# FFNs and output projections with activations held in the array and 512 weight columns streamed, instead of weights held and tokens streamed

## The chip, the core and the metric

One NeuronCore of a Trainium2 chip runs the whole program. The metric is device microseconds of one execution; a comparison takes the median of several. Engines: PE multiplies matrices, DVE (VectorE) and ACT (ScalarE) work on elements, POOL prepares constants, SP issues DMAs. A matmul holds 128 x 128 numbers in the array (the stationary operand, loaded first) and streams the columns of the other (the moving operand) past them; its result goes to PSUM.

## The reference

A trunk of two layers over 256 tokens of 1024 channels, in float32. Layer 0 mixes tokens by latent attention and a spatial gate, layer 1 by a short gated convolution; each mixer stands between two FFNs, so there are four FFNs.

```python
def rms_norm(x, g):
    y = x32 * lax.rsqrt(jnp.mean(x32 * x32, axis=-1, keepdims=True) + NORM_EPS)
    return (y * g.astype(jnp.float32)).astype(x.dtype)

def swiglu(h, w_gate, w_up, w_down):           # 1024 -> 2816 -> 1024
    return (jax.nn.silu(h @ w_gate) * (h @ w_up)) @ w_down

for layer in range(DEPTH):
    x = x + 0.5 * swiglu(rms_norm(x, ffn_pre_norm[layer]), ...)
    h = rms_norm(x, mix_norm[layer])
    x = x + (mla_sgu_mixer(h, ...) if layer % 2 == 0 else short_conv_mixer(h, ...))
    x = x + 0.5 * swiglu(rms_norm(x, ffn_post_norm[layer]), ...)
return rms_norm(x, final_norm)
```

## The kernel before

Activations stay on the chip with channels on partitions and the 256 tokens on the free axis. Every float32 operand of a large product is split into two parts, hi and lo (float32r), and three of the four products of parts are made: hi x hi, hi x lo, lo x hi. ACT makes hi by a copy (`whi`, line 123), DVE makes lo by a subtraction (`wlo`, line 126); the activation's two parts lie side by side as `[hi | lo]`, 512 columns (`mv` for x times a norm's gain, `a` for silu's result).

Weights come in pieces of 1 MB (2048 numbers on each partition) in the order of their use, `plan`. `prefetch` issues a piece's DMA on SP three pieces ahead of its use and splits it; raw, hi and lo have three buffers each.

Where a tile of 128 weight columns is held, `mm` (lines 164 and 165) makes a pair: w_hi against all 512 columns of `[a_hi | a_lo]`, then w_lo against the 256 of a_hi. `mm3` (lines 169 to 171) makes the same as a triple of three 256-column products into one half bank. An FFN (`ffn`) runs over 22 tiles f of 128 hidden channels: `products(f)` makes gate and up (8 tiles of channels x 2 x a pair), then `gate(f - 1)` adds the two halves (`pair_sum`), multiplies by the norm's factor spread over the partitions, applies silu and splits the result into `a[f]`. `project_out` runs four times over 256 output channels: 22 x 2 pairs each, and triples in the last of the four, then adds into x. The mixers' output projections use the same function. A norm takes squares of x (ACT), adds them up (DVE), sums over partitions on PE (line 211), takes the root, and for an FFN spreads the factor again on PE (line 221). At the end x is turned by 16 transposes and written.

One product already stands the other way, with tokens on partitions and 512 weight columns streamed: the gate's v and the attention's values (`natural`, lines 583 to 585).

A scheduler sets each engine's order from the data dependences and priorities (`tc.high_priority()`); an engine then works in that order and waits at whatever is not ready.

Of the kernel before, what the change touches and what calls it, by code (L numbers as in the profile page):

```python
# [63 lines left out]
def trunk(ctx: ExitStack, tc: tile.TileContext, io: dict, out: bass.AP, stop=None):  # L64
# [26 lines left out]
    plan += [io["e_out"][c] for c in range(4)]  # L91
# [4 lines left out]
    plan += [io["c_out"][c] for c in range(4)]  # L96
# [4 lines left out]
    def prefetch(n):  # L101
        while len(ready) < min(n, len(plan)):
            src = plan[len(ready)]
            w = src.shape[1]
# [4 lines left out]
            cuts = [0, 256, 512, 1024, 1536, w] if n == 0 else list(range(0, w, 512)) + [w] if n == 1 else [0, w]  # L109
            pieces = list(zip(cuts, cuts[1:]))  # L110
            for a, b in pieces:
                if n == 0:
                    k0, k1 = a // 256, b // 256
                    c = k0 // 2
                    nc.sync.dma_start(x[c][:, k0 - 2 * c:k1 - 2 * c, :], io["xT"][:, k0:k1, :])
                nc.sync.dma_start(raw[:, a:b], src[:, a:b])
            for a, b in pieces:
                if n == 0:
                    for k in range(a // 256, b // 256):
                        split_to(mv[k], x[k // 2][:, k % 2, :], col(C_PRE0 + k))  # L120
                for q in range(a, b, HI_STEP):
                    e = slice(q, min(q + HI_STEP, b))
                    A.activation(hi[:, e], raw[:, e], AF.Copy)  # L123
                for q in range(a, b, LO_STEP):
                    e = slice(q, min(q + LO_STEP, b))
# [11 lines left out]
    # ---------------------------------------------------------------- input, small parameters  # L137
    small = const.tile([P, NCOL], F32, name="small")
    x = [const.tile([P, 2, T], F32, name=f"x{c}") for c in range(4)]
# [27 lines left out]
    def mm3(ps, hi, lo, m, first, last):  # L167
        """All three products into ps[:, 0:256]."""
# [4 lines left out]
    def split_to(m, src, scale=None):  # L173
        """m = [hi | lo] of src (times a per-partition scale)."""
# [6 lines left out]
    def rsqrt(v, name):  # L181
        """v ** -0.5 in [P, 2], to float32's accuracy."""
# [13 lines left out]
    def after(later, earlier):  # L196
        """`later` is issued behind `earlier` on their engine."""
# [4 lines left out]
    def norm_split(c, gcol):  # L202
        """mv of x[c]: x * gain, split."""
        return [split_to(mv[k], x[c][:, k % 2, :], col(gcol + k)) for k in (2 * c, 2 * c + 1)][1]

    def total(accs, behind=None):
        """Sums over partitions (channels), the tokens on partitions: [P, 2]."""
# [9 lines left out]
    def spread(rn, behind=None):  # L217
        """[P, 2] of the tokens -> [P, T] in PSUM, the same on every partition."""
# [8 lines left out]
    def refine(root, h, y):  # L227
        """y = 1 / root, one Newton step further; h: -0.5 * what the root is of."""
# [7 lines left out]
    def rms(ps):  # L236
# [3 lines left out]
        A.activation(root, ps, AF.Sqrt, scale=1.0 / D, bias=eps)  # L240
# [138 lines left out]
    if stop == "f0":  # L379
        return dump()  # L380
# [422 lines left out]
```

## Time and profile before

| | us |
|---|---|
| median of 3 runs | 948.96 |
| lowest and highest | 947.68, 949.72 |
| the profiled execution, first to last instruction (span) | 949.5 |
| PE busy | 934.3 |
| DVE busy | 705.7 |
| ACT busy | 539.2 |

The page gives for the profiled execution its span alone, 0.5 us above the median of the runs. Busy times of PE are lengths of matmuls that overlap, so that PE looks busy even where it does not run at its best; the distance between two starts tells more. A group's row by form gives the count, the busy time, the mean length in ns, and the idle time before it with what ended that.

### The profile page before, as it was taken

How to read it: one execution, taken by the hardware profiler on the slowest of the kernel's cores; microseconds unless marked ns; L12 is line 12 of the kernel's file. 1: busy time of each engine (PE TensorE's matmuls, PEld its weight loads, DVE VectorE, ACT ScalarE, POOL GpSimd, SP SyncE). 2: the span in 40 equal slices, each digit the busy share in tenths (PEclk: the TensorE clock that was granted, in tenths of full speed). 3: DMA queues.
4: the chain of work that ended last, by engine and by line, in shares of the span. 5: the costliest groups of instructions: out<-in, count | busy, mean ns of one | idle time of the engine just before them, and what ended most of it. 6: DMA issues, size and time to landing. Idle time of an engine off the chain costs nothing.

```text
span 949.5 us, 14524 instructions
## 1 busy us (share of the span) xinstructions
PE 934.3 (98%) x5692; PEld 830.5 (87%) x5692; DVE 705.7 (74%) x1344; ACT 539.2 (57%) x827; POOL 4.6 (0%) x13
## 2 busy tenths in 40 slices
PE   7999999999999999999999999999999999999997
PEld 6888888998979888888998888889888888888887
DVE  6998775667778888775677887666788977788552
ACT  7655554554766655655456556554555665655542
POOL 0000000001000000000000000000000000000000
PEclk9999999999999999999999999999999999999999
DMA  8754455545415455555545555555455465555631
GB/s 278 275 208 178 177 193 174 197 170 177 178 49 190 177 206 178 183 195 174 203 178 188 205 184 181 196 173 205 178 183 208 149 214 177 188 205 174 200 122 45
DMA packets 26996, 173.60 MB, mean 183 GB/s; under 512 B 3120, under 2 KB 3760, under 8 KB 8240
## 3 DMA queue, kind: packets, MB, share of 16 engines
q1 hardware_dynamic: 26928, 172.68, 52.1%
q8 instruction: 44, 0.72, 0.3%
q14 instruction: 24, 0.20, 0.1%
HBM read 171.62 MB, written 1.05 MB: 182 GB/s over the span
## 4 chain that ended last, share of the span: by engine, by line
PE 96%; DVE 1%; ACT 1%; DMA 1%; SPq 0%; issue 0%; DVEq 0%; ACTq 0%
PE ps L164 53%; PE ps L165 27%; PE psb L171 3%; PE psb L170 3%; PE psb L169 3%; PE ps L170 1%; PE ps L171 1%; PE ps L169 1%; DMA x<-in_xT 1%; PE ps L583 0%; PE ps L584 0%; PE ps L585 0%; DVE wlo L126 0%; PE ps L651 0%; PE psb L221 0%; PE ps L673 0%
## 5 line engine op out<-in xcount | busy, mean ns | idle before, releaser
L126 DVE TENSOR_TENSOR wlo<-raw,whi 128x512 fp32r<-128x512 f32 (+1 forms) x647 | 430.6, 686 | 188.9 <-ACT whi L123 188.7
L164 PE MATMUL ps<-mv,whi 128*128 128x512 f32 x1600 | 561.9, 395 | 6.1 <-DVE mv L179 5.0
L123 ACT ACTIVATE whi<-raw 128x1024 fp32r<-128x1024 f32 (+2 forms) x337 | 337.9, 1018 | 213.1 <-PE ps L164 99.0
L165 PE MATMUL ps<-mv,wlo 128*128 128x256 f32 x1600 | 449.8, 281 | 0.3 <-DVE wlo L126 0.3
L164 PEld LDWEIGHTS ps<-mv,whi 128*128 128x128 f32 x1600 | 300.9, 188 | 74.3 <-ACT whi L123 6.6
L165 PEld LDWEIGHTS ps<-mv,wlo 128*128 128x128 f32 x1600 | 303.4, 190 | 1.2 <-DVE wlo L126 1.0
L164 PE MATMUL ps<-a,whi 128*128 128x512 f32 x624 | 218.0, 393 | 0.1
L165 PE MATMUL ps<-a,wlo 128*128 128x256 f32 x624 | 174.9, 281 | 0.0
L164 PEld LDWEIGHTS ps<-a,whi 128*128 128x128 f32 x624 | 116.9, 187 | 26.7 <-DVE a L177 0.4
L165 PEld LDWEIGHTS ps<-a,wlo 128*128 128x128 f32 x624 | 117.9, 189 | 0.2 <-issue 0.2
L359 ACT ACTIVATE silu<-pt 128x256 f32<-128x256 f32 x88 | 36.7, 418 | 95.3 <-DVE pt L357 95.3
L295 DVE TENSOR_TENSOR pt<-ps,sb 128x512 f32<-128x512 f32 x96 | 65.6, 683 | 0.5 <-ACT sb L294 0.4
L357 DVE TENSOR_TENSOR pt<-pt,r 128x512 f32<-128x512 f32 x88 | 60.2, 684 | 5.4 <-ACT r L270 5.3
L176 ACT ACTIVATE a<-pt 128x256 fp32r<-128x256 f32 x88 | 36.8, 418 | 41.8 <-DVE pt L360 41.8
L294 ACT ACTIVATE sb<-ps 128x512 f32<-128x512 f32 x100 | 58.1, 581 | 1.9 <-PE ps L165 1.9
L171 PE MATMUL psb<-a,wlo 128*128 128x256 f32 x208 | 58.8, 283 | 0.0
L170 PE MATMUL psb<-a,whi 128*128 128x256 f32 x208 | 58.8, 283 | 0.0
L169 PE MATMUL psb<-a,whi 128*128 128x256 f32 x208 | 58.8, 283 | 0.0
L169 PEld LDWEIGHTS psb<-a,whi 128*128 128x128 f32 x208 | 39.9, 192 | 0.3
L171 PEld LDWEIGHTS psb<-a,wlo 128*128 128x128 f32 x208 | 39.9, 192 | 0.0
L170 PEld LDWEIGHTS psb<-a,whi 128*128 128x128 f32 x208 | 39.9, 192 | 0.0
L177 DVE TENSOR_TENSOR a<-pt,a 128x256 fp32r<-128x256 f32 x88 | 36.9, 419 | 2.3 <-ACT a L176 2.2
(186 smaller groups left out, 546.0 us busy)
## 6 DMA issues: line engine op xcount, KB each, us to landing
raw<-in_f_gu SPq DMA_DIRECT2D x86, 1024.0 KB, 4.8
raw<-in_f_dn SPq DMA_DIRECT2D x32, 1024.0 KB, 4.9
raw<-in_f_dn SPq DMA_DIRECT2D x16, 768.0 KB, 4.2
raw<-in_c_cz SPq DMA_DIRECT2D x8, 1024.0 KB, 4.9
raw<-in_e_in SPq DMA_DIRECT2D x7, 1024.0 KB, 4.8
raw<-in_e_out SPq DMA_DIRECT2D x4, 1024.0 KB, 4.8
raw<-in_c_b SPq DMA_DIRECT2D x4, 1024.0 KB, 4.7
raw<-in_c_out SPq DMA_DIRECT2D x4, 1024.0 KB, 4.8
```

The costliest lines, as they stand in the source:

```text
L123: A.activation(hi[:, e], raw[:, e], AF.Copy)
L126: V.tensor_tensor(lo[:, e], raw[:, e], hi[:, e].bitcast(F32), ALU.subtract)
L164: PE.matmul(ps, lhsT=hi, rhs=m, start=first, stop=False)
L165: return PE.matmul(ps[:, :T], lhsT=lo, rhs=m[:, :T], start=False, stop=last)
L169: PE.matmul(ps, lhsT=hi, rhs=m[:, :T], start=first, stop=False)
L170: PE.matmul(ps, lhsT=hi, rhs=m[:, T:], start=False, stop=False)
L171: PE.matmul(ps, lhsT=lo, rhs=m[:, :T], start=False, stop=last)
L176: return (A.activation(m[:, :T], src, AF.Copy), V.tensor_tensor(m[:, T:], src, m[:, :T].bitcast(F32), ALU.subtract))
L177: V.tensor_tensor(m[:, T:], src, m[:, :T].bitcast(F32), ALU.subtract))
L294: A.activation(sb, ps[:, :, T:], AF.Copy)
L295: V.tensor_tensor(t, ps[:, :, :T], sb, ALU.add)
L357: V.tensor_tensor(t, t, bc(r[0], 2), ALU.mult)
```

## The change

In the four FFNs and the two output projections the operands change places: a 128-token half of the activations is held in the array, and 512 weight columns stream past. Results then have tokens on partitions. `mm_b` makes three products of 512 columns: a_hi with w_hi, a_hi with w_lo, a_lo with w_hi. `products(c)` now makes two tiles f at once (11 steps c), each with its own half of tokens in a PSUM bank; silu takes the norm's factor as a scale for each partition, and `gate` transposes the result on PE before it is split into `a`. x lies with tokens on partitions; `Norm.block` transposes each 512-column block of x as it comes out of `project_out`, splits it into `mv`, and takes its squares with a sum along the row. `project_out` holds four banks, keeps its last two pieces (TAIL) and finishes one block after the other. A piece of weights has the same size, but is cut over two tiles f and four tiles k, or over four groups of 256 columns. One instruction of DVE now splits 1024 columns, not 512.

```diff
-LOOKAHEAD = 3
-HI_STEP, LO_STEP = 1024, 512      # columns that one instruction splits
+LOOKAHEAD = 3
+TAIL = 2
+STEP = 1024
+NC = NF // 2
...
+    def down_plan(src, order):
+        v = src.rearrange("c p n -> p c n")
+        for i in order:
+            plan.append(v[:, :, i * 512:(i + 1) * 512])
...
-        for f in range(NF):
-            plan.append(io[f"{tag}_gu"][f])
-        for c in range(4):
-            for k0, k1 in ((0, 8), (8, 16), (16, 22)):
-                plan.append(io[f"{tag}_dn"][c][:, k0 * 256:k1 * 256])
+        v = io[f"{tag}_gu"].rearrange("f p n -> p f n")
+        for c in range(NC):
+            for h in range(2):
+                plan.append(v[:, 2 * c:2 * c + 2, h * 1024:(h + 1) * 1024])
+        down_plan(io[f"{tag}_dn"], range(NC))
...
+        def squares(self, h, b):
+            junk = work.tile([P, 512], F32, name="junk", tag="sq")
+            A.activation(junk, x[h][:, b * 512:(b + 1) * 512], AF.Square, accum_out=self.ss[:, b, h:h + 1])
+
+        def block(self, h, b):
+            if self.gcol is not None:
+                ps = psB.tile([P, 512], F32, name="psb")
+                for i in range(4):
+                    PE.transpose(ps[:, i * P:(i + 1) * P], x[h][:, b * 512 + i * P:b * 512 + (i + 1) * P], ident)
+                for i in range(4):
+                    k = 4 * b + i
+                    src, m, g = ps[:, i * P:(i + 1) * P], mv[k], col(self.gcol + k)
+                    hi, lo = m[:, h * P:(h + 1) * P], m[:, T + h * P:T + (h + 1) * P]
+                    A.activation(hi, src, AF.Copy, scale=g)
+                    V.scalar_tensor_tensor(lo, src, g, hi.bitcast(F32), ALU.mult, ALU.subtract)
+            self.squares(h, b)
...
+    def mm_b(ps, a, w, first, last):
+
+        PE.matmul(ps, lhsT=a[0], rhs=w[0], start=first, stop=False)
+        PE.matmul(ps, lhsT=a[0], rhs=w[1], start=False, stop=False)
+        PE.matmul(ps, lhsT=a[1], rhs=w[0], start=False, stop=last)
...
+        for i in order[:-TAIL]:
+            ws[i] = weights()
+            for h in range(2):
+                for b in range(2):
+                    step(i, h, b)
+        for i in order[-TAIL:]:
+            ws[i] = weights()
+        for b in range(2):
+            for h in range(2):
+                for i in order[-TAIL:]:
+                    step(i, h, b)
+                with tc.high_priority():
+                    xs = x[h][:, b * 512:(b + 1) * 512]
+                    V.scalar_tensor_tensor(xs, ps[h][:, b, :], s, xs, ALU.mult, ALU.add)
+                    norm.block(h, b)
...
+        def gate(c, ps):
+            s = work.tile([P, 2, 2, P], F32, name="silu")
+            for h in range(2):
+                v = ps[:, h, :].rearrange("p (f j n) -> p f j n", f=2, j=2)
+                A.activation(s[:, h], v[:, :, 0, :], AF.Silu, scale=rn[:, h:h + 1])
+                V.scalar_tensor_tensor(s[:, h], v[:, :, 1, :], rn[:, h:h + 1], s[:, h], ALU.mult, ALU.mult)
+            pt = psB.tile([P, 512], F32, name="psb")
+            for f in range(2):
+                for h in range(2):
+                    o = (2 * f + h) * P
+                    PE.transpose(pt[:, o:o + P], s[:, h, f, :], ident)
+            hi, lo = a[c]
+            A.activation(hi, pt, AF.Copy)
+            V.tensor_tensor(lo, pt, hi.bitcast(F32), ALU.subtract)
```

At the start x is turned by 16 transposes into the new lie. At the end the final norm needs no transposes: the gains are spread over the partitions once (`gain`, made by PE among the convolution's first products), and DVE multiplies x by factor and gain in four instructions, one for each output DMA.

Three places in the order of the built programs. First, PE in the middle of an FFN, where the products of one step end (on `mv7`) and those of the next begin (on `mv0`). Before:

```order
L165 MATMUL ps_1048<-mv6_101,wlo_987 128x256
L164 MATMUL ps_1048<-mv7_102,whi_986 128x512
L165 MATMUL ps_1048<-mv7_102,wlo_987 128x256
L164 MATMUL ps_1048<-mv7_102,whi_986 128x512
L165 MATMUL ps_1048<-mv7_102,wlo_987 128x256
L164 MATMUL ps_1101<-mv0_95,whi_1039 128x512
```

Now, the operand named first being the one that is streamed:

```order
L317 MATMUL ps_2760<-whi_2672,mv6_103 128x512
L315 MATMUL ps_2760<-whi_2672,mv7_104 128x512
L316 MATMUL ps_2760<-wlo_2673,mv7_104 128x512
L317 MATMUL ps_2760<-whi_2672,mv7_104 128x512
L315 MATMUL ps_2760<-whi_2672,mv7_104 128x512
L316 MATMUL ps_2760<-wlo_2673,mv7_104 128x512
L317 MATMUL ps_2760<-whi_2672,mv7_104 128x512
L374 MATMUL psb_2830<-ident_90,silu_2825 128x128 x4
L315 MATMUL ps_2837<-whi_2704,mv0_97 128x512
```

All products are of 512 columns now, and four transposes of the step before last stand between two steps.

Second, PE at the seam from the second FFN to the third: the last products of the down projection (on `a20`, `a21`) and the first of the next FFN (on `mv0`). Before:

```order
L169 MATMUL psb_4660<-a21_3083,whi_4641 128x256
L170 MATMUL psb_4660<-a21_3083,whi_4641 128x256
L171 MATMUL psb_4660<-a21_3083,wlo_4642 128x256
L164 MATMUL ps_4855<-mv0_95,whi_4650 128x512
L165 MATMUL ps_4855<-mv0_95,wlo_4651 128x256
```

Now:

```order
L315 MATMUL ps_3466<-whi_3692,a20_2603 128x512
L316 MATMUL ps_3466<-wlo_3693,a20_2603 128x512
L317 MATMUL ps_3466<-whi_3692,a21_2604 128x512
L315 MATMUL ps_3906<-whi_3724,mv0_97 128x512
L316 MATMUL ps_3906<-wlo_3725,mv0_97 128x512
L317 MATMUL ps_3906<-whi_3724,mv0_97 128x512
L315 MATMUL ps_3906<-whi_3724,mv1_98 128x512
L275 MATMUL psb_3868<-ident_90,x1_81 128x128 x4
L316 MATMUL ps_3906<-wlo_3725,mv1_98 128x512
```

The transposes of the last block of x (`x1`) stand four products into the next FFN; those of the three blocks ahead of it stand among the last products of the down projection.

Third, ACT at the same seam. Before, splits of x (`mv`, 256 columns) and squares (`sq`) among the splits of weights (`whi`):

```order
L123 ACTIVATE whi_4846<-raw_4845 128x1024 x2
L178 ACTIVATE mv6_101<-x3_83,small_79 128x256
L123 ACTIVATE whi_4889<-raw_4888 128x1024
L178 ACTIVATE mv7_102<-x3_83,small_79 128x256
L279 ACTIVATE sq_4820<-x3_83 128x512
```

Now (`psb` is the transposed block, `junk` takes the squares, `root` is the norm's root):

```order
L280 ACTIVATE mv4_101<-psb_3840,small_79 128x128
L139 ACTIVATE whi_3756<-raw_3755 128x1024
L280 ACTIVATE mv5_102<-psb_3840,small_79 128x128
L139 ACTIVATE whi_3756<-raw_3755 128x1024
L280 ACTIVATE mv6_103<-psb_3840,small_79 128x128
L269 ACTIVATE junk_3881,ss_2582<-x1_81 128x512
L280 ACTIVATE mv4_101<-psb_3868,small_79 128x128
L139 ACTIVATE whi_3764<-raw_3763 128x1024
L251 ACT_TABLE_LOAD
L251 ACTIVATE root_4038<-sst_4036,eps_95 128x2
L280 ACTIVATE mv5_102<-psb_3868,small_79 128x128
```

Twice as many splits of half the size, in the order in which the two halves of the tokens come, and the root with its table stands among them.

## Rows read from the trace of the kernel before

**Rows 1.** The page, parts 1 and 4: engines' busy time; chain that ended last.

```profile
PE 934.3 (98%) x5692; PEld 830.5 (87%) x5692; DVE 705.7 (74%) x1344; ACT 539.2 (57%) x827; POOL 4.6 (0%) x13
...
PE 96%; DVE 1%; ACT 1%; DMA 1%; SPq 0%; issue 0%; DVEq 0%; ACTq 0%
```

**Rows 2.** Groups by line and form: count | busy us, mean ns | idle before.

```profile
L164 PE MATMUL ps<-mv,whi 128*128 128x512 f32 x1600 | 561.9, 395 | 6.1 <-DVE mv L179 5.0 <-ACT whi L123 1.2
...
L164 PE MATMUL ps<-a,whi 128*128 128x512 f32 x624 | 218.0, 393 | 0.1
...
L169 PE MATMUL psb<-a,whi 128*128 128x256 f32 x208 | 58.8, 283 | 0.0
```

**Rows 3.** Windows, line 164: PE busy (count), weight loads, granted clock, DMA share.

```profile
20.00:180.00 160.00, 159.68 (x453) 84.93 (x452) 1.00 0.58 203
500.00:640.00 140.00, 140.00 (x405) 75.54 (x404) 1.00 0.54 190
```

**Rows 4.** Timeline of PE, last triples: start us, length us, engine, line.

```profile
940.06 0.28 PE L169 MATMUL psb<-a,whi 128*128 128x256 f32 x1
...
940.30 0.28 PE L171 MATMUL psb<-a,wlo 128*128 128x256 f32 x1
```

**Rows 5.** Timeline of PE, the gate's v: steps 1, 7 and 22.

```profile
215.69 0.40 PE L583 MATMUL ps<-whi,mv 128*128 128x512 f32 x1
...
217.08 0.39 PE L583 MATMUL ps<-whi,mv 128*128 128x512 f32 x1
...
220.48 0.39 PE L583 MATMUL ps<-whi,mv 128*128 128x512 f32 x1
```

**Rows 6.** Timeline of PE, attention: transposes (line 673) between 512-column products.

```profile
258.68 0.39 PE L585 MATMUL ps<-wlo,a 128*128 128x512 f32 x1
258.94 0.30 PE L673 MATMUL ps<-ident,sm 128*128 128x128 f32 x1
258.99 0.48 PE L583 MATMUL ps<-whi,a 128*128 128x512 f32 x1
259.31 0.71 PE L673 MATMUL ps<-ident,sm 128*128 128x128 f32 x5
259.78 0.47 PE L584 MATMUL ps<-whi,a 128*128 128x512 f32 x1
260.09 0.39 PE L585 MATMUL ps<-wlo,a 128*128 128x512 f32 x1
```

**Rows 7.** Timeline of PE, second FFN: norm sum (line 211) between pairs.

```profile
302.65 0.28 PE L165 MATMUL ps<-mv,wlo 128*128 128x256 f32 x1
302.77 0.50 PE L211 MATMUL psb<-ones,nacc 128*128 128x1 f32 x4
...
303.45 0.28 PE L165 MATMUL ps<-mv,wlo 128*128 128x256 f32 x1
```

**Rows 8.** Groups by line and form, DVE and ACT, columns as in rows 2.

```profile
L126 DVE TENSOR_TENSOR wlo<-raw,whi 128x512 fp32r<-128x512 f32 x645 | 429.8, 687 | 188.5 <-ACT whi L123 188.4
L123 ACT ACTIVATE whi<-raw 128x1024 fp32r<-128x1024 f32 x310 | 323.1, 1055 | 213.1 <-PE ps L164 99.0 <-issue 94.9 <-PE ps L170 14.4
...
L246 ACT ACT_TABLE_LOAD x9 | 11.5, 1283 | 2.2 <-DVE rn L233 2.1
...
L661 ACT ACTIVATE sm<-ps,nm 128x128 f32<-128x128 f32 x8 | 3.0, 370 | 0.1
```

**Rows 9.** The page, parts 2 and 6: GB/s by slice; DMA to landing.

```profile
GB/s 278 275 208 178 177 193 174 197 170 177 178 49 190 177 206 178 183 195 174 203 178 188 205 184 181 196 173 205 178 183 208 149 214 177 188 205 174 200 122 45
...
raw<-in_f_gu SPq DMA_DIRECT2D x86, 1024.0 KB, 4.8
```

**Rows 10.** Timeline of PE: first pair behind the last wait at the start.

```profile
14.45 0.39 PE L164 MATMUL ps<-mv,whi 128*128 128x512 f32 x1
```

**Rows 11.** Timelines of DVE and SP at the end: output multiplications, DMA issues.

```profile
943.56 1.41 DVE L467 TENSOR_SCALAR o<-ps,rn 128x512 f32<-128x512 f32 x2
...
944.26 1.81 SPq L470 DMA_DIRECT2D out<-o  x4
```

More of the change, by code (lines that the diff above doesn't have):

```diff
@@ L90, in trunk @@
         plan.append(io[name][i])
-    plan += [io["e_out"][c] for c in range(4)]
+    down_plan(io["e_out"], (2, 3, 0, 1))
     ffn_plan("f1")
@@ L281, in sumsq_step, with widen @@
+    def widen(rn, behind=None):
+        r = work.tile([P, T], F32, name="r")
+        A.activation(r, spread(rn, behind), AF.Copy)
+        return r
     def sumsq_step(acc, s, i):
@@ new lines, in mv_part, with project_out, step @@
+    def mv_part(k, h):
+        return mv[k][:, h * P:(h + 1) * P], mv[k][:, T + h * P:T + (h + 1) * P]
+    def project_out(stat, order, s, norm):
+        ps = [psA.tile([P, 2, 512], F32, name="ps") for h in range(2)]
+        ws = {}
+        def step(i, h, b):
+            for f in range(2):
+                w = [t.rearrange("p (c k n) -> p c k n", c=4, k=2)[:, 2 * b:2 * b + 2, f, :] for t in ws[i]]
+                mm_b(ps[h][:, b, :], stat(2 * i + f, h), w, i == order[0] and f == 0, i == order[-1] and f == 1)
+        for i in order[:-TAIL]:
[13 more added lines that the diff above has]
+                    norm.block(h, b)
@@ new lines, in ffn, with products, stat @@
+    def ffn(norm, then):
+        a = [[act.tile([P, 512], F32R, name=f"a{2 * c + i}") for i in range(2)] for c in range(NC)]
+        def products(c):
+            ps = psA.tile([P, 2, 512], F32, name="ps")
+            for b in range(2):
+                w = [t.rearrange("p (f k n) -> p f k n", f=2, k=4) for t in weights()]
+                steps = [(h, i) for h in range(2) for i in range(4)] if c == 0 else \
+                        [(h, i) for i in range(4) for h in range(2)]
+                for h, i in steps:
+                    k = 4 * b + i
+                    mm_b(ps[:, h, :], mv_part(k, h), [t[:, :, i, :] for t in w], k == 0, k == KD - 1)
+            return ps
+        def gate(c, ps):
[5 more added lines that the diff above has]
+            pt = psB.tile([P, 512], F32, name="psb")
+            for f in range(2):
+                for h in range(2):
[4 more added lines that the diff above has]
+            V.tensor_tensor(lo, pt, hi.bitcast(F32), ALU.subtract)
+        rn = None
+        before = products(0)
+        for c in range(1, NC):
+            ps = products(c)
+            if c == 1:
+                with tc.high_priority():
+                    rn = norm.factor()
+                    load_table(AF.Silu, rn[:, 0:1])
+            gate(c - 1, before)
+            before = ps
+        gate(NC - 1, before)
+        def stat(k, h):
+            o = (2 * (k % 2) + h) * P
+            return [t[:, o:o + P] for t in a[k // 2]]
+        project_out(stat, list(range(NC)), 0.5, then)
@@ new lines, in y_part @@
+    def y_part(y):
+        return lambda k, h: (y[k][:, h * P:(h + 1) * P], y[k][:, T + h * P:T + (h + 1) * P])
+    norm = Norm(C_PRE0)
+    prefetch(2)
+    for b in range(2):
+        for h in range(2):
+            ps = psB.tile([P, 512], F32, name="psb")
+            for i in range(4):
+                PE.transpose(ps[:, i * P:(i + 1) * P], xt[2 * b + i // 2][:, i % 2, h * P:(h + 1) * P], ident)
+            A.activation(x[h][:, b * 512:(b + 1) * 512], ps, AF.Copy)
+            norm.squares(h, b)
@@ new lines, in trunk @@
+    then = Norm(C_MIX0)
+    ffn(norm, then)
+    norm = Norm(C_POST0)
+    mixer_even(ctx, tc, locals(), then, norm)
+    then = Norm(C_PRE1)
+    ffn(norm, then)
+    norm = Norm(C_MIX1)
+    ffn(then, norm)
+    gain = const.tile([P, D], F32, name="gain", tag="vn")
+    for b in range(2):
+        ps = psB.tile([P, 512], F32, name="psb")
+        for i in range(4):
+            c = C_FIN + 4 * b + i
+            PE.matmul(ps[:, i * P:(i + 1) * P], lhsT=small[:, c:c + 1].broadcast_to([P, P]), rhs=ident,
+                      start=True, stop=True)
+        V.tensor_copy(gain[:, b * 512:(b + 1) * 512], ps)
@@ L408, in trunk @@
         if r is None:
-            r = fin.spread(fin())
+            r = widen(norm.factor())
             r2 = const.tile([P, T], F32, name="r2", tag="rr")
@@ L424, in trunk @@
         split_to(y[j], yt)
-    project_out(y, list(range(KD)), ((0, 8),), 1.0)
-    if stop == "m1":
-        return dump()
-    ffn(C_POST1)
-    acc = work.tile([P, 2, T], F32, name="nacc", bufs=1)
-    xg = [act.tile([P, 2, T], F32, name=f"xg{c}", tag=f"mv{c}") for c in range(4)]
-    for c in range(3):
-        square_step(acc, c)
-    V.tensor_tensor(acc[:, 0, :], acc[:, 0, :], acc[:, 1, :], ALU.add)
-    load_table(AF.Sqrt, acc[:, 0, 0:1])
-    sq = work.tile([P, 2, T], F32, name="sq")
-    for j in range(2):
-        A.activation(sq[:, j, :], x[3][:, j, :], AF.Square)
@@ L473, in mixer_even @@
-def mixer_even(ctx, tc, env):
+    norm = Norm(C_POST1)
+    project_out(y_part(y), list(range(4)), 1.0, norm)
+    then = Norm(None)
+    ffn(norm, then)
+    load_table(AF.Sqrt, then.ss[:, 0, 0:1])
+    rn = then.factor()
+    for h in range(2):
+        for b in range(2):
+            e = slice(b * 512, (b + 1) * 512)
+            o = act.tile([P, 512], F32, name=f"o{h}{b}", tag=f"mv{2 * h + b}")
+            V.scalar_tensor_tensor(o, x[h][:, e], rn[:, h:h + 1], gain[:, e], ALU.mult, ALU.mult)
+            nc.sync.dma_start(out[h * P:(h + 1) * P, e], o)
```

206 lines of the change are left out of this document (42 added, 164 removed).

## The prediction

> **What bounds the kernel now.** I read the page's busy shares and its chain first: PE is busy for 934.3 of 949.5 us and 96% of the chain that ended last is PE [rows 1]. DVE and ACT come behind at 74% and 57%. So a microsecond counts only if it shortens or lengthens the row of instructions on PE, or opens a hole in it. Since matmuls overlap, their mean lengths (395 ns for 512 columns) don't add up; what adds up is the distance from one start to the next, so the second thing I read is steps. The list by form gives the counts: 2,224 pairs of a 512- and a 256-column product (1600 + 624), and 208 triples of 256 columns [rows 2]. 192 of the pairs are the convolution's input projection and stay; the other 2,032 and all the triples are what is turned round.
>
> A pair has two gaits. From 20 to 180 us 452 steps take 160 us, 0.353 us each; from 500 to 640 us 404 take 140 us, 0.3465 [rows 3]. I count the first FFN (484 pairs, 13 of them before steady running) at the slow gait and the rest at the quick one. In a triple each 256-column product takes a step of 0.12 us [rows 4], so 0.36.
> Before: 471 x 0.353 + 1,561 x 0.3465 + 208 x 0.36 = 166.3 + 540.9 + 74.9 = 782.1 us.
>
> **The turned products.** The kernel before has one place that runs them in the new form: the gate's v, with tokens on partitions and 512 weight columns streamed (lines 583 to 585). Its first six steps take 1.39 us (0.232 each), the next fifteen 3.40 us (0.2267) [rows 5]. Columns and multiplications stay the same, so there are (2,032 x 768 + 208 x 768) / 512 = 3,360 such products: 3,360 x 0.2267 = 761.7 us. The turn is worth 782.1 - 761.7 = **20.4 us**, since a matmul costs its columns and a fixed 13 ns, and there are fewer of them. I take 0.2267 because the new rows stand 48 in a row, far beyond the six in which the old place settled; the other bound, 0.232 throughout, is a rival below. New is that a moving operand is two runs of 256 columns, which no matmul of before has; I price it at nothing, and the same rival holds it.
> [...] The rows have 227 and 120, a fixed part of 13 ns, and I go by them.
>
> **The transposes, new on PE's path.** Silu's result now has tokens on partitions, and the down projection needs it turned: 4 transposes for each of 11 x 4 pairs of tiles, 44 groups. Each end of a stage that feeds a norm turns x for the next one: 5 x 4 groups. They stand in PE's row between products (first two order listings), so nothing hides them. The price is read in the attention: from 258.68 to 260.09 three 512-column products and six transposes in two places take 1.41 us, so the transposes cost 1.41 - 3 x 0.227 = 0.73, 0.122 each with their entries [rows 6]; a group of 4 is 0.49. 64 x 0.49 = **+31.4 us**. Bounds: 0.11 each (five last 0.71 us, the last of them 0.27) gives 28.2; the price of a lone one (258.68 to 259.31 is 0.63 for two products and one transpose, so 0.18) would give 46.
>
> **What PE loses and gains besides.** The norm's sums over partitions and their spreading go: four FFNs lose two groups of four, the two mixers one. One group holds 0.80 us where a pair alone holds 0.35 [rows 7]: 10 x 0.45 = **-4.5 us**. The table of final gains adds 16 passes at 0.11, **+1.8**.
> So PE's row: -20.4 + 31.4 - 4.5 + 1.8 = +8.3 us.
>
> **The other engines in the steady part.** In two pieces of weights (11.4 us of PE) ACT has four splits of 1,024 columns at 1.06, two silus and a copy, under 6 us; DVE has four subtractions of 1,024 columns, at most 2 x 0.69 each, and three small ones, about 7 [rows 8]. Pair sums and the multiplication by the widened factor are gone. Both stay under PE, so what they save is worth nothing. SP issues one DMA for each piece as before; the pieces are the same 1 MB but come in runs of 2 or 4 KB. One lands 4.8 us after its issue [rows 9] and PE uses one in 24 x 0.227 = 5.4, with three pieces in flight: hidden. If that cover went, each late microsecond of a piece would be PE's.
>
> **The start.** Before, 13 pairs have begun when PE starts the one at 14.45 us and runs on [rows 10]: 9.9 us lost. Now the first result needs 2 MB of weights instead of 1, beside the same 1 MB of x, at the 278 GB/s of the first slice [rows 9]: at most 3.7 us later. Sixteen transposes of x come in (2.0 us, partly in holes), and two of their PSUM tiles wait for ACT's copies, behind which the next split is queued. Between 0 and +5.7 I take **+2.5**.
>
> **The seams.** Each block of 512 columns of x passes DVE (one addition), PE (four transposes), ACT and DVE (four splits of 128 columns) and ACT (squares). PE's transposes of the last block are queued 4 products behind it (second listing): 0.91 us, against the last product's end and DVE's addition of 0.69, so 0.1 to 0.3 is waited. On ACT the new work of a seam is 4 x (4 x 0.37 + about 0.8) = 9.1 us, beside two pieces of weights (4.2) and two table loads (2.6) [rows 8]: 16, from the first block's end to the use of the last split tile some 19 us later. It fits narrowly; behind it queue the splits of the next weights, for which PE waits. Six seams: **+1** (0 to 10).
>
> **The end.** The factor's chain is about as long as before (the transposes behind it go, a row of squares stays). But the four last multiplications now run on DVE alone, 0.70 each [rows 11]: the last is ready 2.8 us after the first begins, where SP's four issues were through 2.5 us after it (943.56 to 946.07). With that issue of 0.45 itself **+0.7** (-0.5 to +1.5).
>
> **The sum.** +8.3 + 2.5 + 1 + 0.7 = +12.5 us. The profiled execution's span is 949.5, 0.5 over the median of the runs; on the median 948.96 + 12.5 = 961.5 us. The change buys a denser stream and pays more for transposes than it gets.
>
> **Rivals.**
> *Faster: the fixed 13 ns shrink.* The new order puts the two products with the same stationary half side by side. [...] It decides for faster once the step is under 0.2267 - 12.5 / 3,360 = 0.223. Against it: the triples already run two products in a row from the same weights, and their step is 0.12 all the same, 107 ns of columns and 13 [rows 4]. [...] 0.08.
> *The stream never settles,* through the groups between or the split moving operand: 0.2317 throughout is 3,360 x 0.005 = +16.8, 978 us. For it: the first six steps [rows 5]. Against: 15 quiet ones behind them. 0.12.
> *ACT becomes the bound at the seams.* If a split takes 0.5 instead of 0.37 and waits for freed weight buffers pile up, about 1.5 us a seam over mine: 969 us. 0.13.
> *A transpose costs its length.* At 0.27 [rows 6], 256 are 69 us instead of 31.4: 999 us. [...] 0.02.
> *No change.* The start fills its holes, the seams are free, and groups cost 0.36: 0.05.
>
> **How the numbers follow.** My forecast has 0.60. Its own bounds (groups at 0.44, start and seams at their ends) are 953 to 967. The range goes up to the seams' case and part of the way to the stream's, 952 to 975; outside it lie the faster case, the long transposes and most of the slow stream. Within 0.2% (1.9 us) I take as no change, about what can be measured here: faster 0.08, same 0.06, slower 0.86.
>
> **What would show it.** Starts of the new products 0.227 apart in mid-FFN; a group of four transposes that makes 0.49 us between them; one FFN of 186.9 us (792 x 0.2267 + 15 x 0.49); PE without waits over 0.3 us but at the start. [...]

## The result

The changed kernel takes 963.27 us in the median of four runs (962.89 to 963.93), the kernel before 948.32 us beside it (947.44 to 949.72): a ratio of 1.0153, with an interval of 1.013 to 1.0175. It is slower, and inside the range that was given. Measured again later, it is 964.07 against 948.43 us, 1.016 (1.014 to 1.0179).

The page of the changed kernel, its busy shares and the chain that ended last, against [rows 1]:

```profile
PE 942.2 (98%) x4588; PEld 785.1 (82%) x4588; DVE 564.3 (59%) x800; ACT 486.4 (51%) x736; POOL 5.3 (1%) x13
...
PE 96%; DVE 1%; ACT 1%; DMA 1%; SPq 0%; issue 0%; DVEq 0%; ACTq 0%
PE ps L317 27%; PE ps L315 27%; PE ps L316 26%; PE ps L179 5%; PE ps L180 2%; PE psb L374 2%; PE ps L184 1%; PE ps L185 1%; PE ps L186 1%; PE psb L275 1%; DMA raw<-in_f_gu 1%; PE ps L587 0%; PE ps L589 0%; PE ps L588 0%; PE ps L655 0%; DVE wlo L140 0%
```

PE has 1,104 instructions fewer and is busy 8 us longer. DVE went from 74% to 59% and ACT from 57% to 51%, and that bought nothing: the chain is PE at 96%, as before.

The timeline of PE in the middle of the second FFN (start us, length us, engine, line, out<-in):

```profile
368.09 0.48 PE L315 MATMUL ps<-whi,mv 128*128 128x512 f32 x1
...
369.56 0.39 PE L315 MATMUL ps<-whi,mv 128*128 128x512 f32 x1
...
378.85 0.39 PE L317 MATMUL ps<-whi,mv 128*128 128x512 f32 x1
379.08 0.60 PE L374 MATMUL psb<-ident,silu 128*128 128x128 f32 x4
379.43 0.48 PE L315 MATMUL ps<-whi,mv 128*128 128x512 f32 x1
```

From 369.56 to 378.85 there are 41 steps in 9.29 us, 0.2266 each. From the product behind one group of transposes to the product behind the next it is 379.43 - 368.09 = 11.34 us: 48 products make 10.88 (48 x 0.2267), so a group of four transposes makes 0.46. The second FFN takes 186.87 us from its first product (299.95) to the first of the third (486.82). 186.9 was forecast.

Where the spans' difference of 11.7 us (949.5 to 961.2) arises, read as the distance from the first product of one stage to that of the next:

| stage | before | after | difference |
|---|---|---|---|
| start and first FFN, to the mixer | 197.53 | 200.29 | +2.76 |
| mixer with its output projection | 98.17 | 99.66 | +1.49 |
| second FFN | 184.71 | 186.87 | +2.16 |
| third FFN | 184.71 | 186.89 | +2.18 |
| conv's input projection (with the table of gains) | 67.68 | 69.72 | +2.04 |
| conv's output projection | 22.91 | 23.25 | +0.34 |
| fourth FFN to the end | 193.80 | 194.51 | +0.71 |

Nothing is concentrated in one place. The list of PE's waits confirms it; here are all that it has (engine, line, awaited, us in total, times, longest):

```profile
PE ps L315 <- ACT whi L130: 6.3, 2, 5.3
PE psb L232 <- DVE skvn L244: 1.1, 1, 1.1
PE psb L687 <- ACT vn L710: 0.9, 1, 0.9
PE ps L316 <- DVE wlo L131: 0.8, 1, 0.8
PE ps L677 <- DVE sm L670: 0.4, 1, 0.4
PE psb L687 <- ACT pT L679: 0.4, 1, 0.4
```

The two waits of lines 315 and 316 are the start; lines 232, 677 and 687 are the mixer's small steps. None belongs to a seam or to the middle of an FFN. The groups of the other engines, by line and form, answer to [rows 8] (count | busy us, mean ns | idle before):

```profile
L139 ACT ACTIVATE whi<-raw 128x1024 fp32r<-128x1024 f32 x318 | 320.7, 1052 | 322.4 <-issue 167.4 <-PE ps L317 131.9 <-PE ps L185 13.9
L140 DVE TENSOR_TENSOR wlo<-raw,whi 128x1024 fp32r<-128x1024 f32 x318 | 376.8, 1222 | 305.1 <-ACT whi L139 305.1
...
L374 PE MATMUL psb<-ident,silu 128*128 128x128 f32 x176 | 27.1, 273 | 0.0
```

Both engines idle some 300 us ahead of their splits. A transpose is 273 ns long, but [rows 6] was right that its length is not its price.

### The profile page after: what moved, and what is told of

It reads as the page before. It is cut to its first block, busy times and chain, and to the rows that moved or that the text cites. A ratio compares the mean times of both kernels' runs of the same rounds, so it can differ in the third digit from the quotient of the medians.

```text
span 961.2 us, 11528 instructions
## 1 busy us (share of the span) xinstructions
PE 942.2 (98%) x4588; PEld 785.1 (82%) x4588; DVE 564.3 (59%) x800; ACT 486.4 (51%) x736; POOL 5.3 (1%) x13
## 4 chain that ended last, share of the span: by engine, by line
PE 96%; DVE 1%; ACT 1%; DMA 1%; SPq 0%; issue 0%; DVEq 0%; ACTq 0%
PE ps L317 27%; PE ps L315 27%; PE ps L316 26%; PE ps L179 5%; PE ps L180 2%; PE psb L374 2%; PE ps L184 1%; PE ps L185 1%; PE ps L186 1%; PE psb L275 1%; DMA raw<-in_f_gu 1%; PE ps L587 0%; PE ps L589 0%; PE ps L588 0%; PE ps L655 0%; DVE wlo L140 0%
## 5 line engine op out<-in xcount | busy, mean ns | idle before, releaser
L140 DVE TENSOR_TENSOR wlo<-raw,whi 128x1024 fp32r<-128x1024 f32 x320 | 378.5, 1220 | 305.1 <-ACT whi L139 305.1
L139 ACT ACTIVATE whi<-raw 128x1024 fp32r<-128x1024 f32 x320 | 321.8, 1050 | 322.4 <-issue 167.4
L315 PE MATMUL ps<-whi,mv 128*128 128x512 f32 x704 | 279.2, 397 | 6.3 <-ACT whi L130 6.3
L316 PE MATMUL ps<-wlo,mv 128*128 128x512 f32 x704 | 275.6, 391 | 0.8 <-DVE wlo L131 0.8
L317 PE MATMUL ps<-whi,mv 128*128 128x512 f32 x704 | 275.4, 391 | 0.0
L315 PE MATMUL ps<-whi,a 128*128 128x512 f32 x416 | 163.4, 393 | 0.0
L317 PE MATMUL ps<-whi,a 128*128 128x512 f32 x416 | 162.6, 391 | 0.0
L315 PEld LDWEIGHTS ps<-whi,mv 128*128 128x128 f32 x704 | 132.8, 189 | 33.4 <-ACT whi L130 7.2
L317 PEld LDWEIGHTS ps<-whi,mv 128*128 128x128 f32 x704 | 132.7, 188 | 28.0
L179 PE MATMUL ps<-mv,whi 128*128 128x512 f32 x192 | 67.0, 395 | 0.0
L180 PE MATMUL ps<-mv,wlo 128*128 128x256 f32 x192 | 53.1, 279 | 0.0
L179 PEld LDWEIGHTS ps<-mv,whi 128*128 128x128 f32 x192 | 35.9, 188 | 7.9
L180 PEld LDWEIGHTS ps<-mv,wlo 128*128 128x128 f32 x192 | 36.1, 188 | 0.6 <-DVE wlo L140 0.4
```

Of the source, the lines that this page charges most:

```text
L140: V.tensor_tensor(lo[:, e], raw[:, e], hi[:, e].bitcast(F32), ALU.subtract)
L179: PE.matmul(ps, lhsT=hi, rhs=m, start=first, stop=False)
L180: return PE.matmul(ps[:, :T], lhsT=lo, rhs=m[:, :T], start=False, stop=last)
L315: PE.matmul(ps, lhsT=a[0], rhs=w[0], start=first, stop=False)
L316: PE.matmul(ps, lhsT=a[0], rhs=w[1], start=False, stop=False)
L317: PE.matmul(ps, lhsT=a[1], rhs=w[0], start=False, stop=last)
```

## The experiments

**Without the gate's transposes.**

```diff
-            pt = psB.tile([P, 512], F32, name="psb")
-            for f in range(2):
-                for h in range(2):
-                    o = (2 * f + h) * P
-                    PE.transpose(pt[:, o:o + P], s[:, h, f, :], ident)
+            pt = s.rearrange("p h f n -> p (h f n)")
```

> The changed kernel without the gate's 44 groups of four transposes: the split for the down projection takes silu's result as it stands (tokens on partitions), so what is multiplied there is not the reference's product; all else is as changed. Theory (PE's row of steps is the bound, a group costs 0.46 us between products): 963.3 - 44 x 0.46 = 943 us, faster than the kernel before by about 0.5%; one FFN from its first product to the next stage 181.8 us instead of 186.9. Rival A (the groups are mostly hidden, and the loss comes from the start, the seams and scattered waits): at most 5 us less, 958 or more. Rival B (without transposes the next bound appears, ACT or the weights' landing): products in mid-FFN further apart than 0.227 us, total between 945 and 955.

941.72 us, 0.9909 of the kernel before (0.9891 to 0.9927). One FFN is 181.59 us where it was 186.87, so 11 groups cost 5.28 us, 0.48 each with what hangs on the last one. From the timeline of PE:

```profile
360.99 0.39 PE L315 MATMUL ps<-whi,mv 128*128 128x512 f32 x1
...
371.87 0.39 PE L315 MATMUL ps<-whi,mv 128*128 128x512 f32 x1
```

48 steps in 10.88 us, across the border between two tiles, and no wait in its place. Without these transposes the turned kernel is faster than the kernel before, with them it is slower: the theory holds, both rivals fall. How much faster depends on which execution of the kernel before it is held against (see below): 0.9% by the medians, 0.5% against one of the quickest (spans of 941.2 and 946.3 us).

**Only the down and output projections turned.** Gate and up run as before:

```diff
+                for j in range(2):
+                    o = (2 * k + j) * P
+                    p = mm(ps[:, j, :], hi[:, o:o + P], lo[:, o:o + P], mv[k], k == 0, k == KD - 1)
...
-        project_out(stat, list(range(NC)), 0.5, then)
+        project_out(y_part(a), list(range(NC)), 0.5, then)
```

> Only the down and output projections are turned round (x with tokens on partitions, transposes of x at each seam, 20 groups); gate and up keep the order of the kernel before, weights held. Theory (costs add up stage by stage): an FFN is 352 x 0.3465 + 264 x 0.2267 + 4 x 0.46 + one spreading of the factor 0.45 = 184.1 us, against 184.7 before; with the dearer output projections (+1.2), table of gains (+1.8), mixer (+0.6) and a start about 1 us later: 950 to 953 us, +0.2 to +0.5% on the kernel before. Rival (the two halves depend on each other: without the other half the seams open up, since DVE and ACT have the old gates beside the new splits): waits of PE at the six seams of 1 us or more each, 957 or more.

955.89 us, 1.0066 (1.0047 to 1.0084), 3 us over the theory's end. PE's list of waits has none at a seam, and the second FFN takes 184.51 us, near the 184.1 worked out. But the third takes 186.66. Windows of line 177, the pairs' 512-column product, in the second, third and fourth FFN (window, PE busy (count), granted clock, DMA share, GB/s):

```profile
320.00:410.00 90.00, 90.00 (x260) 1.00 0.55 190
500.00:590.00 90.00, 90.00 (x256) 1.00 0.54 187
780.00:870.00 90.00, 90.00 (x256) 1.00 0.54 187
```

In the same 90 us there are 260 pairs in the second and 256 in the other two: the slow gait of [rows 3] again, 0.353 us a pair, now in other FFNs than the first. 352 pairs x 0.0066 us x 2 = 4.6 us. Without them it would be 951.3, inside the theory's range. A pair's gait was no property of the first FFN.

**Only gate and up turned.** Down, output projections and norms as before:

```diff
+                    p = mm_b(ps[:, h, :], mv_part(k, h), [t[:, :, i, :] for t in w], k == 0, k == KD - 1)
...
+                    PE.transpose(pt[:, o:o + P], s[:, h, f, :], ident)
+            for f in range(2):
+                split_to(a[2 * c + f], pt[:, f * T:(f + 1) * T])
...
         project_out(a, list(range(NF)), ((0, 8), (8, 16), (16, 22)), 0.5)
```

> Only gate and up are turned round (44 groups of transposes of silu's result); down and output projections and the norms keep the order of the kernel before. Theory: an FFN is 528 x 0.2267 + 11 x 0.46 + 0.45 (sum over partitions) + 61.6 (down as before) = 186.8 us and waits as before, 187.0 against 184.7; the start about 3 us later (2 MB of weights for the first result): 956 to 960 us. Together with the run that turns only the other half, the increments over the kernel before should add up to about the whole 15 us. Rival (turned gate and up are no dearer; the loss is in what surrounds the norms): 951 or less.

965.50 us, 1.0164 (1.0144 to 1.0184): 5.5 us over the theory's end, and no faster than both halves together (1.0153 and 1.016; the intervals overlap). Gate and up of the second FFN take 124.87 us, as worked out (125.2). The down projection takes 63.15 us where it took 61.59, and windows of line 173, its 512-column products, show part of why (down projections of the second and of the fourth FFN; columns as above):

```profile
432.00:466.00 34.00, 34.00 (x97) 1.00 0.50 170
...
900.00:930.00 30.00, 30.00 (x88) 1.00 0.55 186
```

34 us hold 96 steps, the slow gait of 0.353; 30 us hold 87, the quick one of 0.346. For 132 pairs that is 0.88 of the 1.56 us; about 0.5 more is, as an estimate, the last group of transposes, which stands behind the border. The first and the third FFN's down take 63.15 and 63.17 us like the second's. Where the rest of the 5.5 us comes from was not taken apart. The increments of the two halves over the kernel before (5.0 and 14.6 us) make 19.6, not 15: the sum of the halves holds only if the gaits are taken out. For the second FFN it does: -0.20 (down alone) + 3.31 (gate and up alone) - 0.88 (132 slow pairs) = 2.2, and the whole change has 2.16.

**x by a second load, gains by a DMA.** 

```diff
-                PE.transpose(ps[:, i * P:(i + 1) * P], xt[2 * b + i // 2][:, i % 2, h * P:(h + 1) * P], ident)
+        nc.sync.dma_start(x[h], io["xn"][h * P:(h + 1) * P, :])
...
-            PE.matmul(ps[:, i * P:(i + 1) * P], lhsT=small[:, c:c + 1].broadcast_to([P, P]), rhs=ident,
+    nc.sync.dma_start(gain, io["fin"].broadcast_to([P, D]))
```

> The changed kernel, with x loaded a second time with tokens on partitions (1 MB more from DRAM, behind the first two pieces of weights) instead of 16 transposes, and the table of gains broadcast by a DMA instead of 16 passes of PE. Theory: the conv stage loses 1.8 us; at the start the transposes (0.213 us each at the low clock, 3.4 us in all, about half of it in holes) go: 1 to 2.5 us. Together 959 to 960.5 us. Rival (the start is set by the landing of 2 MB of weights, and the transposes stood in its holes): 961.5. Third: the 1 MB more of x delays the third piece of weights, for which PE then waits: 962 or more.

960.03 us, 1.0106 (1.0089 to 1.0124). The total is inside the theory. The stage with the first FFN is 1.45 us shorter (198.84), but that is one execution against one, and the start of the changed kernel moves by 2 us between two executions (last experiment). The conv's input projection is only 0.68 us shorter (69.04) instead of 1.8, since its 192 pairs ran at 0.353: the windows of line 179 from 690 to 740 us count 146 in the changed kernel and 143 here.

**The gait itself.** The kernel before with four more groups of small passes in the first FFN:

```diff
+                if gcol == C_PRE0 and f in (2, 3, 4, 5) and k == 6:
+                    spread(r[0], p)
```

> The kernel before with four more spreadings of the factor in the first FFN (in its 3rd to 6th pair of tiles, each four passes of PE whose result nobody reads, 0.45 us). Question: what decides the gait of the pairs (0.353 or 0.3465 us). Theory (two stable gaits with the same instructions; an interruption by other instructions is where a row of pairs can change its gait, and nothing else does): in the trace the gait changes, if it does, only at one of the four groups or at those that were there; 1.8 us dearer, and up to 2.9 cheaper for every switch to the quick gait early in the first FFN: between -1.3 and +1.8 us. Rival (the first FFN is slow for a reason of its own, its x, its buffers or its weights' landing): it stays at 0.353 throughout, +1.8 us. Rival (the gait changes by itself): a change away from any such group.

950.65 us against 950.03, 1.0014 (0.9998 to 1.0029): inside the theory's range, and not to be told from no change. The first FFN ran quick in the profiled execution, so the rival that it is slow for a reason of its own falls. But it was quick from the spreading that was there before, at 21.18 us, and behind each of the four new groups the quick row went on quick. So they can't be credited with it, and an interruption need not change a gait; whether one can had to be seen otherwise.

**Three more executions of the kernel before, unchanged.**

> The kernel before, unchanged, one more profiled execution, to see which rows of pairs run in which gait this time. Theory (the gait of a row of pairs is settled anew at each interruption, in each execution): the pattern of slow and quick stages differs from the first profile, where the first FFN was slow and the other three quick, and the span goes with it: 946.4 us plus 0.0066 us for every pair in the slow gait (352 to 484 pairs, 2.3 to 3.2 us, for an FFN). Rival (the pattern belongs to the program): slow in the first FFN alone, span 949 to 950.

> As the look beside it: the same program once more. Theory: a span of 946.4 us plus 0.0066 for every slow pair, in whatever stages they lie. Rival: slow in the first FFN alone, span 949 to 950.

> As the two looks beside it: the same program once more. Theory: a span of 946.4 us plus 0.0066 for every slow pair, in whatever stages they lie. Rival: slow in the first FFN alone, span 949 to 950.

The three executions took 952.73, 951.28 and 948.06 us, with spans of 951.0, 949.5 and 946.3. The windows of line 164 from 60 to 130 us, first FFN, for the first of them and for the third:

```profile
60.00:130.00 70.00, 70.00 (x199) 1.00 0.52 184
```

```profile
60.00:130.00 70.00, 70.00 (x203) 1.00 0.53 182
```

The second has 199 too, like the execution shown ahead. In two the pattern is the one that the rival expected, but the third refutes it: it is not the program that is slow in its first FFN, but an execution. The sum that was expected with it is about a microsecond too high (947.5 for the third), since its base already held the short slow rows behind the seams. In the third one can see a gait change; its timeline of PE around the spreading of the factor (line 221):

```profile
18.39 0.40 PE L164 MATMUL ps<-mv,whi 128*128 128x512 f32 x1
...
20.51 0.40 PE L164 MATMUL ps<-mv,whi 128*128 128x512 f32 x1
...
21.22 0.60 PE L221 MATMUL psb<-ident,rn 128*128 128x128 f32 x4
21.59 0.48 PE L164 MATMUL ps<-mv,whi 128*128 128x512 f32 x1
21.90 0.28 PE L165 MATMUL ps<-mv,wlo 128*128 128x256 f32 x1
```

The same place in the execution that is shown ahead of the prediction:

```profile
18.41 0.40 PE L164 MATMUL ps<-mv,whi 128*128 128x512 f32 x1
...
20.49 0.40 PE L164 MATMUL ps<-mv,whi 128*128 128x512 f32 x1
...
20.84 0.60 PE L221 MATMUL psb<-ident,rn 128*128 128x128 f32 x4
21.20 0.48 PE L164 MATMUL ps<-mv,whi 128*128 128x512 f32 x1
21.52 0.28 PE L165 MATMUL ps<-mv,wlo 128*128 128x256 f32 x1
```

Six pairs ahead of the group take 2.12 us in the third execution, 0.353 each, and behind it the row goes on in the quick gait. In the other they take 2.08 us, 0.347 each, and the row goes on in the slow one, to its last pair at 181 us. The first product behind the group takes 0.31 us in one and 0.32 in the other: a hundredth of a microsecond there goes with 3 us later.

What goes with the gait of a long row is thus to be seen ahead of it. Between the norm's sums (line 211) and the spreading stand ten pairs. In these four executions and the run with four more groups there are 20 such places, one for each FFN: in 17 the ten pairs are slow and the long row behind is quick, in 3 the ten are quick and the long row is slow. The three are the first FFNs of the execution shown ahead and of the first and second here; the other three FFNs have ten slow pairs and a quick row each time. That is no rule for any interruption: behind the four new groups of the run above, with 16 pairs between them, quick stayed quick, and in the run with only the down projections turned, where what stands ahead is different, two of these FFNs were slow.

The span of the third execution is 3.2 us below that of the second. By the excess of every pair over 0.3467 us, the second has some 590 slow pairs and the third 170: 420 x 0.0066 = 2.8. The first has as many slow pairs as the second, and is 1.4 us longer already at the end of gate and up in the first FFN. That is its start: its 14th pair begins at 15.99 us, that of the second at 14.63.

**The pairs regrouped.** If 512 and 256 in alternation beat, another order might not:

```diff
+        for j, o in enumerate(os):
+            PE.matmul(ps[:, j, :], lhsT=hi[:, o:o + P], rhs=m, start=first, stop=False)
+        for j, o in enumerate(os):
+            p = PE.matmul(ps[:, j, :T], lhsT=lo[:, o:o + P], rhs=m[:, :T], start=False, stop=last)
```

> The kernel before with the products of two column tiles regrouped: 512, 512, 256, 256 columns (both high halves, then both low ones) where 512, 256, 512, 256 stood, in gate and up, in the down and output projections and in half of the conv's input projection; nothing is turned round and no operation is added or dropped. Theory (the slow gait is a beat of 512 and 256 in alternation): a regrouped quartet takes 2 x 0.2267 + 2 x 0.120 = 0.693 us everywhere, which is the quick gait; against a kernel before with one slow FFN 3 us less, against one whose FFNs are all quick nothing: 946 to 948 us on a chip where before has 948 to 952, and with less scatter. Rival (the slow gait belongs to mixed widths in any order): no change, 948 to 952. Rival (two 256-column products in a row don't cover the load for a 512 one): a dearer quartet, 0.72 or more, 20 us and more slower.

951.18 us against 950.03, 1.001 (0.9996 to 1.0024). Windows of its line 169, first and third FFN:

```profile
60.00:130.00 70.00, 63.07 (x202) 1.00 0.55 190
...
500.00:570.00 70.00, 63.15 (x202) 1.00 0.54 194
```

One gait in the long rows, 0.6966 us a quartet. That is 0.3483 a pair, between the two old ones: the slow gait is gone and the quick one too. Twelve runs lie between 950.34 and 953.17, 29 of the kernel before between 947.35 and 953.05. The theory has half: without the alternation there is one gait (the run below has the same 0.6966), but the new order does not have the quick step.

**The cheaper half, with everything that seemed free.** Down turned, regrouped, second load of x, gains by DMA:

> Only the down and output projections turned, as in the run with that half alone (955.9 us), with gate and up regrouped as in the run beside this one, x loaded a second time with tokens on partitions instead of 16 transposes, and the gains broadcast by a DMA. Theory (sums of steps): 955.9 less 2 x 2.3 for two FFNs that fell into the slow gait, less 1.8 for the gains, less 1 for the start: 948 to 949 us, about as fast as the kernel before and 1 to 2 us behind the regrouped one. Rival (the slow gait survives the regrouping): 952 to 953.

954.81 us, 1.0045 (1.0031 to 1.0059): 6 us over the theory. Regrouping costs 4 x 352 x 0.0018 = 2.5 us against the quick gait. Most of the rest lies in the stage with the first FFN, 198.04 us where the run with the down projections alone has 195.20. What is new there besides the regrouping is the second load of x, which was harmless in the turned kernel. Here PE waits for the norm's factor (from that x), and then for the third piece's splits, which ACT makes behind a table load that stands behind that factor. Its waits, and its windows at the start (PE, PEld, DVE, ACT, POOL busy (count), granted clock, DMA share, GB/s):

```profile
PE psb L237 <- DVE rn L249: 1.6, 1, 1.6
...
PE ps L182 <- ACT whi L137: 0.9, 1, 0.9
```

```profile
20.00:23.00 3.00, 0.92 (x5) 0.76 (x6) 1.02 (x3) 2.97 (x5) 0.00 (x0) 1.00 0.95 398
23.00:26.00 3.00, 2.47 (x10) 1.77 (x10) 3.00 (x3) 3.00 (x5) 0.00 (x0) 0.76 0.12 39
```

After waits of 1.6, 0.9 and 0.5 us PE goes on with a granted clock of 0.76 in the mean of the window, which has 10 products in 2.47 us. No version here that makes all of the work beats the kernel before. The best mixture is only an estimate, which no run shows: the down-turned half with every FFN quick, 955.9 - 4.6 = 951.3, or 949.5 with the gains by DMA, against 948.06 for the kernel before with every FFN quick.

**The changed kernel once more.**

> The changed kernel, unchanged, timed once more on the same chip as the looks at the kernel before. Theory (its 3,360 turned products have one gait, and only the conv's 192 pairs two): a range of runs within 1.5 us, where the kernel before ranges over 4 to 5; the profile's FFNs 186.9 us again; 12 to 14 us slower than before. Rival (the scatter has another source than the gaits): the same range for both.

964.07 us, 1.016 (1.014 to 1.0179). The FFNs repeat (186.92 and 186.88), but the runs lie between 960.99 and 964.93: the theory that a single gait means little scatter falls. The profiled execution, 963.2 us, is 2.0 longer than the first one. All of that is gone through by the mixer (202.33 against 200.29); from there to the end the two differ by 0.01. So it is the start. Timeline of PE in the first execution:

```profile
8.88 1.91 PE L407 MATMUL psb<-ident,xt 128*128 128x128 f32 x8
11.72 0.50 PE L315 MATMUL ps<-whi,mv 128*128 128x512 f32 x1 [0.94 <-ACT whi L130]
12.98 0.50 PE L316 MATMUL ps<-wlo,mv 128*128 128x512 f32 x1 [0.76 <-DVE wlo L131]
...
16.82 0.63 PE L317 MATMUL ps<-whi,mv 128*128 128x512 f32 x1
17.24 0.56 PE L315 MATMUL ps<-whi,mv 128*128 128x512 f32 x1
17.64 0.40 PE L316 MATMUL ps<-wlo,mv 128*128 128x512 f32 x1
```

And in the second:

```profile
8.80 1.43 PE L407 MATMUL psb<-ident,xt 128*128 128x128 f32 x8
12.40 0.51 PE L315 MATMUL ps<-whi,mv 128*128 128x512 f32 x1 [2.17 <-ACT whi L130]
...
19.38 0.61 PE L316 MATMUL ps<-wlo,mv 128*128 128x512 f32 x1
19.81 0.42 PE L317 MATMUL ps<-whi,mv 128*128 128x512 f32 x1
```

The third cut of weights and its split came 0.7 us later. The steps of 0.427 us, against 0.2267 in the steady row, then lasted until 19.8 instead of 17.2 us; the granted clock is 0.53 from 14 to 17 us and 0.90 from 17 to 20 in the first execution, 0.50 and 0.53 in the second. So a delay of 0.7 us cost 2.0. The delay is paid twice here: as a wait (2.17 us instead of 0.94), and in steps of 0.427 us behind it.

## Why the prediction was right, and where it was not

**The direction and its reason hold.** The turned stream is faster than the old one and the transposes take more than it gives. Without the gate's groups the changed kernel would be 0.9% faster than before instead of 1.5% slower.

**The turned products.** 0.2267 us a step was forecast, and it stands in every FFN: neither the rival of 0.2317 throughout nor that of a shrinking fixed part, a step under 0.223, came true. Two steps of 256 columns make 2 x 0.12 = 0.24 [rows 4], the 41 steps of 512 columns are 0.2266 in the mean: so the fixed part is still 13 ns, as an estimate from these two widths.

**The transposes.** 0.49 a group was forecast. Measured were 0.46 between two steps and 0.48 for each of the 11 of an FFN. What then is left of an FFN beside its products, 181.59 - 792 x 0.2267 = 2.0 us, is four groups of x with what hangs on them, 0.51 each. 44 x 0.48 + 20 x 0.51 = 31.3 us, and 31.4 was forecast. The rival that a transpose costs its length is out: the rows' 273 ns are no price between products.

**The start.** This term was mis-sized. +2.5 was forecast, about +4.1 came: before, 9.9 us were lost until the steady row [rows 10]; now the 17th product starts at 17.64, where 16 x 0.2267 = 3.6 us would do, so 14.0 are lost. The step took the bytes and the transposes into account. It left out that PE's steps were long behind the holes: it stood still for 0.94 and 0.76 us, the granted clock from 14 to 17 us is 0.53, and the six products from 14.54 to 17.24 took 0.45 each, against 0.2267 from 17.64 on. In the table the stage shows only +2.76, since the old first FFN ran in its slow gait.

**The seams and the end.** +1 and +0.7 were forecast. The list of waits has none at a seam; the largest gap there is 0.3 us, at the conv's first products. From the start of the last product to the end it is 9.33 us against 9.21. Norm sums gone and gains added came out as forecast: the FFN is 186.87, and the conv's stage +2.04 with 1.8 for the table. The mixer's small steps, now in another order, cost about 0.6 that the sum did not have.

**The anchor was the step that failed.** The sum was made against the profiled execution (span 949.5), as it should be, and came within a microsecond of the difference of the spans (12.5 against 11.7). That it came so close is in part luck: the start and the mixer were 1.6 and 0.6 us dearer than forecast, the end 0.6 cheaper, the seams showed no wait where 1 us was put, and some 590 pairs of the execution shown ahead were slow where 471 were counted (0.8 us). Then it was put on the median of the runs, as if that were the same execution. It was not. In every later run that gave both, the time is 1.7 to 2.1 us over its span (951.28 and 949.5, 962.89 and 961.2). By that the execution shown ahead was, as an estimate, one of about 951.2 us and slow in its first FFN, while the runs' median belongs to quicker ones. Against an execution with four quick FFNs (span 946.3) the changed kernel is 961.2 - 946.3 = 14.9 us slower, and the medians say 15.0. The prediction saw both gaits in [rows 3] and took the slow one for the first FFN's own; it should have asked whether it would be there next time. 471 x 0.0065 = 3.1 us were counted as a gain of the change, and are one only in executions that are slow there. Two bounds were also added up wrongly: start at +5.7 and seams at +10 give about 974, not 967, and 1.5 us at each of six seams 970.5, not 969.

**What stays open.** Why ten slow pairs ahead of the spreading go with a quick row behind it, and ten quick ones with a slow row, is not shown; neither is what settles the gait of the ten, nor why in the changed kernel the landing of the third cut differs between executions.

## What to carry over

When a kernel is bound by the row of TensorE's steps, count starts, not lengths, and ask of every change of lie what has to be turned back: here 2,032 pairs and 208 triples became 3,360 products and gained some 17 to 20 us, while 256 transposes at 0.115 to 0.13 us cost some 31. Before a sum is made, ask whether the profiled execution is the one that the median describes: a second profiled execution of the same program tells. A wait at the start cost more than its length here: 0.7 us of delay in the changed kernel went with 2.0 us, since the products behind it stepped by 0.427 us until 19.8 instead of 17.2 us.

## What the runs showed of the hardware

- A row of alternating 512- and 256-column products ran in one of two gaits here, 0.3467 and 0.353 us a pair. In the third execution of the kernel before it left one for the other at the four small passes at 21.22 us (0.353 ahead, 203 pairs in 70 us behind), and in [rows 3] it kept one for 160 us. In 20 of 20 places the long row behind the spreading had the gait that the ten pairs ahead of it did not have. Regrouped as 512, 512, 256, 256 its long rows had one, 0.3483. Products of 512 columns alone step by 0.2267 in the changed kernel and in the run without the gate's transposes.
- Four transposes of 128x128 float32 are 273 ns long each and cost 0.115 us each between products (0.46 a group in the second FFN of the changed kernel); at its start, where a product of 512 columns steps by 0.43 us (8.45 to 8.88), they stand 0.213 apart.
- The profile's granted clock did not always go with the steps. Windows of the same stretch, ahead of its last three figures, which are granted clock, DMA share and GB/s, the busy times of the engines; first the changed kernel, then the run with x loaded twice:

```profile
14.00:16.00 2.00, 2.00 (x10) 1.71 (x9) 1.58 (x3) 2.00 (x6) 0.00 (x0) 0.54 1.01 411
```

```profile
14.00:16.00 2.00, 2.00 (x7) 1.51 (x5) 1.59 (x4) 1.49 (x2) 0.00 (x0) 1.00 1.02 416
```

  Both step by 0.427 us for 512 columns there, and only one reads 0.54. In the second run the first steps of 0.23 us come at 16.7. The changed kernel reads 1.00 too from 8 to 11 us, where its products step by 0.43; its first shorter step of 512 columns is 0.34, at 12.98. In these two runs the figure reads 1.00 over long steps until the steps have first been short. So the low clock that was expected for the 16 transposes of the start (0.213 us each) is an estimate from their steps: over the first eight the window reads 1.00.
- A piece of an FFN's weights that is read in runs of 2 or 4 KB lands 5.2 us after its issue in the changed kernel (median of 86), against 4.8 in [rows 9]; in neither does PE wait for splits of weights behind the start.
